# Low halves of split weights: an accumulating DMA in place of a subtraction

## The chip, the cores and the metric

The kernel runs on one core of a Trainium2 chip. The metric is device time in microseconds, from launch to end, of the whole program. The profile gives the span from the first to the last instruction of one execution, and times within it are counted from the start of that span.

## The reference

One layer of a bidirectional encoder for an input x of 1024 positions by 1024 channels, float32. The input is RMS-normalised and multiplied with one wide projection matrix; from its columns two branches are fed, an S5 state-space branch (512 channels) and a Hyena branch (1024 channels, two long filters applied in the frequency domain). Both are projected back, merged with sigmoid gates, projected once more, added to x and normalised.

```
xn = rmsnorm(h, norm_w[l])
proj = xn @ w_in[l]
u_s5, g_s5, p_hy, g_hy, m_logits = jnp.split(proj, SPLITS, axis=-1)
y_s5 = s5_mixer(u_s5, g_s5, ...) @ w_branch_s5[l]
y_hy = hyena_mixer(p_hy, g_hy, ...) @ w_branch_hy[l]
m = jax.nn.sigmoid(m_logits)
merged = m[..., :D_MODEL] * y_s5 + m[..., D_MODEL:] * y_hy
h = h + merged @ w_out[l]
return rmsnorm(h, final_norm_w)
```

## The kernel before

Products are made from halves. A float32 tile is split into a high half, which is the value rounded to the matmul format float32r, and a low half, which is the rest; a product is the sum of three passes: high by high, high weight by low input, low weight by high input.

A projection (`proj`, `projs`, line 529) computes 128 output columns for all 1024 positions. Its weights are one column block of 128 columns, taken as 8 blocks of 128 rows (4 for `s5_w_glu` and `w_branch_s5`). It has 16 matmuls in each of three passes (8 with 4 blocks), in the order high weight with `xh`, high weight with `xl`, low weight with `xh`; all go into one PSUM tile `pps`, of which there are two. There are 76 such column blocks, in the order that `weight_pools` (line 490) writes down: the S5 inputs and gates, the merge gates, the Hyena inputs, and the output matrices of the branches.

`prefetch` (line 502) keeps two column blocks ahead of use. For each it loads the raw block (`wraw`, 512 KB or 256 KB, three buffers, SyncE's queue), makes the high half on ScalarE (`whi`, line 510) and the low half by a subtraction (`wlo`, line 513). `whi` and `wlo` have two buffers each, so the halves of one block can be written when the block two before has been used. The subtraction is on GpSimd, except for nine of the last blocks, where it is on VectorE.

The stages, in the order of the span: the Hyena filters (to about 240 us, without projections), S5 inputs and the parameters of the S5 recurrence, four S5 blocks (`s5_block`, mostly VectorE, with projections in between on TensorE), the end of the S5 branch (`s5_tail`, with the small projections), the first forward transform (`hy_forward0`), the first inverse (`hy_inverse0`), the second forward (`hy_forward1`), the second inverse (`hy_inverse1`) and the output. In the transforms the planner weaves projections into the transform's own matmuls. `load_ic` (line 593) loads the constants of an inverse transform, 4 MB, when the forward transform's buffers are free.

The order of the instructions on each engine is not that of the program text: `tile.TileContext(nc, schedule_with_timeline_sim=True)` chooses it from priorities (program order) and from estimated times. At run time every engine and every queue works in that fixed order, and waits at the head of its queue.

Of the kernel before, what the change touches and what calls it, by code (L numbers as in the profile page):

```python
# [12 lines left out]
ALU = mybir.AluOpType  # L13
AF = mybir.ActivationFunctionType
# [86 lines left out]
class Trunk:  # L101
# [400 lines left out]
    def prefetch(self):  # L502

        nc = self.nc
        while (len(self.weights) < 2 or self.w_more) and self.order:
            name, c, nk = nxt = self.order.pop(0)
            raw = self.wr.tile([128, nk, 128], F, name="wraw")
            nc.sync.dma_start(out=raw, in_=self.I[name][0, :, c * 128:c * 128 + 128].rearrange("(k p) c -> p k c", p=128))
            hi, lo = self.w_more.pop() if self.w_more else self.weight_tiles(nk)
            nc.scalar.copy(out=hi, in_=raw)  # L510
            left = len(self.order)
            eng = nc.vector if left < 18 and left % 2 else nc.gpsimd
            eng.tensor_tensor(out=lo, in0=raw, in1=hi, op=ALU.subtract)  # L513
            self.weights.append((nxt, hi, lo))

    def weight_tiles(self, nk):
# [967 lines left out]
```

## Time and profile before

| | |
|---|---|
| median of 3 runs | 1487.98 us (1487.8 to 1488.49) |
| the profiled execution | 1488.18 us |
| its span, first to last instruction | 1486.4 us |
| mean granted TensorE clock | 0.963 of full speed |
| TensorE busy | 1358.1 us, 91% |
| VectorE busy | 1100.0 us, 74% |
| ScalarE busy | 447.0 us, 30% |
| GpSimd busy | 486.4 us, 33% |

Busy shares are means over stages with different limits; what a change in one stage is worth is read in that stage. In the rows PE is TensorE, DVE is VectorE, ACT is ScalarE, POOL is GpSimd, SP is SyncE; a name with a q behind it is that engine's queue. L513 is line 513 of the kernel.

### The profile page before, as it was taken

The numbers are of one execution on the slowest core, as the hardware profiler recorded it, in microseconds if no ns is written. First come the engines' busy times: TensorE is split into PE (matmuls) and PEld (weight loads), VectorE is DVE, ScalarE is ACT, GpSimd is POOL, SyncE is SP. The second block draws the span as 40 slices with busy tenths as digits, with TensorE's granted clock in tenths as the row PEclk, the third lists the DMA queues.
The fourth block names the chain that finished last, engine by engine and source line by source line (L and its number), as shares of the span: only waits on it lengthen the run. The fifth ranks groups of instructions, "written<-read, shape, count | busy, mean of one in ns | idle before, by whom it ended". The sixth has DMA issues, their size and how long they took to land. (4 is left out here: it accounts for less than half of the span.)

```text
span 1486.4 us, 19375 instructions
## 1 busy us (share of the span) xinstructions
PE 1358.1 (91%) x7219; PEld 1143.8 (77%) x7219; DVE 1100.0 (74%) x1963; ACT 447.0 (30%) x661; POOL 486.4 (33%) x306
## 2 busy tenths in 40 slices
PE   5888999998988989899999998999999944999998
PEld 3767888786867868688888776888888844978886
DVE  7999996899789887525479998454569994943532
ACT  4666662122222122232121211333321112511322
POOL 3756764114111111234223312245412111333222
PEclk9998999999999999899999999999999976999999
DMA  8221224622652323243853345645477669633432
GB/s 270 86 71 72 106 86 158 170 86 71 216 160 77 86 74 74 78 143 116 276 182 114 128 140 188 191 158 167 156 267 265 219 209 314 205 131 112 127 111 75
DMA packets 177673, 220.52 MB, mean 148 GB/s; under 512 B 21853, under 2 KB 142937, under 8 KB 174844
## 3 DMA queue, kind: packets, MB, share of 16 engines
q1 hardware_dynamic: 149212, 153.69, 33.8%
q10 hardware_dynamic: 27792, 62.45, 11.6%
q0 software_dynamic: 576, 3.15, 0.6%
q8 instruction: 57, 0.93, 0.3%
q14 instruction: 36, 0.29, 0.1%
HBM read 147.49 MB, written 76.82 MB: 151 GB/s over the span
## 5 line engine op out<-in xcount | busy, mean ns | idle before, releaser
L513 POOL TENSOR_TENSOR wlo<-wraw,whi 128x1024 fp32r<-128x1024 f32 (+1 forms) x67 | 169.6, 2533 | 588.1 <-PE pps L542 412.4
L542 PE MATMUL pps<-xh,whi 128*128 128x512 f32 x896 | 234.4, 408 | 11.5 <-DVE cv L566 11.5
L542 PE MATMUL pps<-xh,wlo 128*128 128x512 f32 x896 | 228.1, 401 | 0.0
L542 PE MATMUL pps<-xl,whi 128*128 128x512 f32 x896 | 226.0, 399 | 0.0
L542 PEld LDWEIGHTS pps<-xh,whi 128*128 128x128 f32 x896 | 169.9, 194 | 50.1 <-issue 12.3
L542 PEld LDWEIGHTS pps<-xh,wlo 128*128 128x128 f32 x896 | 169.2, 191 | 38.9
L542 PEld LDWEIGHTS pps<-xl,whi 128*128 128x128 f32 x896 | 167.9, 190 | 38.9 <-issue 0.2
L510 ACT CAST whi<-wraw 128x1024 fp32r<-128x1024 f32 (+1 forms) x76 | 74.7, 984 | 348.3 <-PE pps L542 276.1
L404 PE MATMUL po<-sh,fo 128*128 128x256 f32 x512 | 101.4, 292 | 6.0 <-DVE sh L111 5.1
L635 PEld LDWEIGHTS iv<-ic,y 128*128 128x128 f32 x752 | 96.5, 193 | 4.8 <-DVE y L113 2.3
L113 DVE TENSOR_TENSOR y<-yraw,y 128x512 fp32r<-128x512 f32 x64 | 61.7, 979 | 51.5 <-ACT y L109 51.2
L635 PE MATMUL iv<-ic,y 128*128 128x256 f32 (+1 forms) x752 | 98.4, 286 | 1.5 <-DVE y L113 1.5
L404 PEld LDWEIGHTS po<-sh,fo 128*128 128x128 f32 x512 | 84.3, 197 | 8.2 <-DVE sh L111 6.1
L357 POOL TENSOR_TENSOR acc<-acc,sq 128x512 f32<-128x512 f32 x56 | 76.3, 1362 | 25.0 <-ACT sq L342 22.8
L404 PE MATMUL po<-sl,fo 128*128 128x256 f32 x256 | 74.4, 291 | 1.0 <-DVE sl L113 1.0
L109 ACT CAST y<-yraw 128x512 fp32r<-128x512 f32 x64 | 39.3, 620 | 92.3 <-PE iv L635 54.1
L722 DVE TENSOR_TENSOR m<-m 128x512 f32<-128x512 f32 x64 | 53.0, 848 | 0.0
L404 PEld LDWEIGHTS po<-sl,fo 128*128 128x128 f32 x256 | 50.5, 197 | 2.3 <-DVE sl L113 1.5
L686 PE MATMUL fwo<-z,zc 128*128 128x256 f32 x384 | 50.1, 283 | 0.5 <-DVE x L716 0.5
L333 PE MATMUL g<-w3h,ha 128*128 128x512 f32 x64 | 33.0, 516 | 19.1 <-DVE e L338 17.3
L686 PEld LDWEIGHTS fwo<-z,zc 128*128 128x128 f32 x384 | 48.5, 191 | 1.6 <-DVE x L716 0.7
L336 ACT ACTIVATE e<-dec,negt 128x512 f32<-128x512 f32 x64 | 45.2, 716 | 10.6 <-DVE so L350 4.8
(437 smaller groups left out, 2685.1 us busy)
## 6 DMA issues: line engine op xcount, KB each, us to landing
wraw<-w_in SPq DMA_DIRECT2D x56, 512.0 KB, 4.6
kspec<-ko SPq DMA_DIRECT2D x32, 512.0 KB, 3.0
kt<-kspec SPq DMA_DIRECT2D x32, 512.0 KB, 3.3
d_y<-x ACTq DMA_DIRECT2D x32, 512.0 KB, 6.0
yraw<-d_y SPq DMA_DIRECT2D x64, 256.0 KB, 4.8
d_m<-cv ACTq DMA_DIRECT2D x16, 512.0 KB, 2.9
d_z<-z ACTq DMA_DIRECT2D x8, 1024.0 KB, 9.8
z<-d_z SPq DMA_DIRECT2D x8, 1024.0 KB, 10.9
```

The costliest lines, as they stand in the source:

```text
L109: nc.scalar.copy(out=hi, in_=src)
L113: e.tensor_tensor(out=lo, in0=src, in1=hi, op=ALU.subtract)
L333: nc.tensor.matmul(out=ps, lhsT=ha[:, tsl], rhs=w3h, start=True, stop=False)
L336: nc.scalar.activation(out=e, in_=decf, func=AF.Exp, scale=negt[:, tt:tt + 1])
L357: nc.gpsimd.tensor_tensor(out=acc, in0=acc, in1=sq, op=ALU.add)
L404: nc.tensor.matmul(out=po[:, part], lhsT=fo[a][:, 12 * (jj % 2) + b], rhs=sd[4 + i][d][:, part], start=n == 0 and part == 0, stop=n == 11 ...
L510: nc.scalar.copy(out=hi, in_=raw)
L513: eng.tensor_tensor(out=lo, in0=raw, in1=hi, op=ALU.subtract)
L542: nc.tensor.matmul(out=ps[:, hf * 512:hf * 512 + 512], lhsT=w[:, kc], rhs=part(x, kc, hf), start=a == 0 and p == 0 and kc == 0, stop=b == ...
L635: nc.tensor.matmul(out=dst, lhsT=lhsT, rhs=self.ic[b][:, j, cols], start=first, stop=last)
L686: nc.tensor.matmul(out=out, lhsT=zc[a][:, b], rhs=z[:, :, d, zi], start=start and n == 0, stop=stop and n == 3 * len(prods) - 1)
L722: nc.vector.tensor_tensor(out=m[:, part, :, 0], in0=m[:, part, :, 0], in1=m[:, part, :, 1], op=op)
```

## The change

The subtraction is replaced by two steps. ScalarE writes minus the high half into `wlo`, and a DMA on GpSimd's queue adds the raw block to it in place. The choice between VectorE and GpSimd goes away.

```
             nc.scalar.copy(out=hi, in_=raw)
-            left = len(self.order)
-            eng = nc.vector if left < 18 and left % 2 else nc.gpsimd
-            eng.tensor_tensor(out=lo, in0=raw, in1=hi, op=ALU.subtract)
+            nc.scalar.activation(out=lo, in_=hi, func=AF.Copy, scale=-1.0)
+            nc.gpsimd.dma_start(out=lo, in_=raw, accum_op=ALU.add)
             self.weights.append((nxt, hi, lo))
```

## Rows read from the trace of the kernel before

**Rows 1.** Stretches: start:end, length, busy PE PEld DVE ACT POOL, clock, DMA, GB/s.
```profile
345.00:610.00 265.00, 234.46 (x1298) 194.06 (x1297) 232.34 (x288) 56.92 (x70) 51.26 (x15) 0.93 0.37 103
790.00:902.00 112.00, 103.55 (x541) 86.16 (x540) 110.00 (x136) 21.52 (x26) 29.39 (x10) 0.98 0.38 129
902.00:937.00 35.00, 35.00 (x144) 28.07 (x144) 24.59 (x30) 7.92 (x8) 5.35 (x2) 0.95 0.72 236
...
1080.00:1100.00 20.00, 19.78 (x107) 16.67 (x106) 8.81 (x11) 4.48 (x6) 4.21 (x2) 1.00 0.89 319
1144.00:1231.00 87.00, 63.51 (x349) 54.49 (x347) 85.52 (x105) 13.30 (x14) 18.29 (x6) 0.88 0.67 230
1231.00:1248.00 17.00, 0.22 (x1) 0.22 (x2) 3.44 (x4) 0.80 (x2) 1.36 (x1) 0.50 1.04 342
```

**Rows 2.** Line 513, the subtraction: duration in ns min/median/max, first and last start.
```profile
L513 POOL TENSOR_TENSOR wlo<-wraw,whi x67: 1289/2407/11716, 242.2 to 1367.9; 128x1024 fp32r<-128x1024 f32 x55, 128x512 fp32r<-128x512 f32 x12
L513 DVE TENSOR_TENSOR wlo<-wraw,whi x9: 1211/1217/1225, 1030.0 to 1357.6; 128x1024 fp32r<-128x1024 f32 x9
```

**Rows 3.** Timeline of GpSimd: start, duration, instruction, idle time before and its releaser.
```profile
399.64 3.50 POOL L513 TENSOR_TENSOR wlo<-wraw,whi 128x1024 fp32r<-128x1024 f32 x1 [17.02 <-PE pps L542]
...
914.96 2.94 POOL L513 TENSOR_TENSOR wlo<-wraw,whi 128x1024 fp32r<-128x1024 f32 x1 [15.01 <-PE pps L542]
```

**Rows 4.** Timeline of VectorE in the S5 blocks.
```profile
400.80 3.42 DVE L1202 TENSOR_TENSOR di<-di,e 128x1024 f32<-128x1024 f32 x1
...
462.89 1.21 DVE L1202 TENSOR_TENSOR di<-di,e 128x1024 f32<-128x1024 f32 x1
...
583.76 2.28 DVE L1215 TENSOR_TENSOR_SCAN st<-a,dr 64x1023 f32<-64x1023 f32 x1
586.07 4.31 DVE L1217 TENSOR_TENSOR_SCAN st<-a,dr 64x1023 f32<-64x1023 f32 x1
```

**Rows 5.** What TensorE waited for, 330 to 620: total us, times, longest.
```profile
PE s5ps L1236 <- DVE sr L1223: 17.1, 3, 6.6
PE pps L542 <- DVE cv L566: 7.2, 1, 7.2
```

**Rows 6.** Timeline of VectorE in the first forward transform.
```profile
851.59 3.33 DVE L719 TENSOR_TENSOR m<-x,kt 128x1024 f32<-128x1024 f32 x1
...
898.24 2.25 DVE L722 TENSOR_TENSOR m<-m 128x512 f32<-128x512 f32 x1
```

**Rows 7.** The cast of line 510 on ScalarE: duration in ns min/median/max.
```profile
L510 ACT CAST whi<-wraw x76: 613/1052/1058, 241.1 to 1364.0; 128x1024 fp32r<-128x1024 f32 x64, 128x512 fp32r<-128x512 f32 x12
```

**Rows 8.** GpSimd's own DMA issues: busy us, mean ns of one.
```profile
L232 POOL DMA_DIRECT2D fo<-c_fo_hi x2 | 1.3, 632 | 0.0
```

**Rows 9.** DMA issues: queue, count, KB each, median us to landing.
```profile
wraw<-w_in SPq DMA_DIRECT2D x56, 512.0 KB, 4.6
...
wraw<-w_branch_s SPq DMA_DIRECT2D x8, 256.0 KB, 2.7
...
fo<-c_fo_hi POOLq DMA_DIRECT2D x2, 768.0 KB, 7.7
```

**Rows 10.** The chain that ended last, between 1215 and 1265: start, us, what.
```profile
1228.42 1.15 DVE m L720
...
1230.90 6.72 DMA ic<-c_ic_hi_d
1237.64 10.16 DMA yraw<-d_y
```

**Rows 11.** Timeline of TensorE: two small projections, then three large ones.
```profile
707.65 2.02 PE L542 MATMUL pps<-tyh,whi 128*128 128x512 f32 x8
...
713.25 2.02 PE L542 MATMUL pps<-tyh,whi 128*128 128x512 f32 x8
...
910.93 3.89 PE L542 MATMUL pps<-xh,wlo 128*128 128x512 f32 x16
...
933.33 3.66 PE L542 MATMUL pps<-xh,wlo 128*128 128x512 f32 x15
```

## The prediction

> **What bounds the kernel now.** I read the busy time by stage first, then what each engine waited for, then the chain of work that ended last, then single stretches of the timeline. The reader should see three kinds of stage in [rows 1]. From 902 to 937 and from 1080 to 1100 TensorE is saturated and VectorE has room; most of the span is like that. In three stretches it is not: the S5 blocks (345 to 610, TensorE busy 234 of 265 us, VectorE 232), the first forward transform (790 to 902, VectorE 110 of 112) and the second (1144 to 1231, VectorE 85.5 of 87, TensorE 63.5). Last come 17 us in which TensorE does nothing (1231 to 1248) and the DMA engines are full. ScalarE and GpSimd are nowhere near a bound. So work taken from GpSimd is worth only what it returns to VectorE or to TensorE's waits.
>
> It returns something, because the subtraction and VectorE get in each other's way. The subtraction that starts at 399.64 takes 3.50 us against a median of 2.41 [rows 2, 3], and the VectorE instruction that meets it takes 3.42 us; the same line undisturbed takes 1.21 [rows 4]. A scan that meets one takes 4.31 against 2.28 [rows 4]. Between 395 and 590 I count 11 such meetings, the first at 400.80 and the last at 586.07, with an excess of 1.5 to 2.2 us each and 22 us in sum. TensorE waits 24.3 us for VectorE in these blocks and at their end: 17.1 and 7.2 [rows 5].
>
> **What is removed.** 67 subtractions on GpSimd and 9 on VectorE [rows 2].
> S5 blocks: 22 us of VectorE's time go. VectorE's chain of a block and TensorE's waits alternate, so the relief comes through while TensorE still waits (24.3 us); but a faster VectorE will now and then stand before TensorE instead. Bounds 0 and 22; I take 18, because both the relief and the waits are larger than that.
> First forward transform: four subtractions meet VectorE between 842 and 902, the first at 851.59 and the last at 898.24 [rows 6], with an excess of 1.6 to 2.2 us each and 7.5 in sum; TensorE is idle for 8.5 us between 790 and 902 [rows 1]. Bounds 0 and 8.5; I take 6.
> Second forward transform: three VectorE subtractions of 1.22 us lie on a VectorE that is 98% busy [rows 1, 2], 3.6 in sum, and two on GpSimd fall into it, at 2.2 each at most by the meetings above. This chain decides when the constants of the last inverse transform are loaded [rows 10]. Bounds 3.6 and 8; I take 4.6, since these two meet VectorE only in part.
> In the saturated stages the removal is worth nothing: TensorE works there without a gap.
>
> **What is added on ScalarE.** One negated copy per weight tile, priced as the cast beside it: 1.05 us for eight blocks, 0.61 for four [rows 7]. 64 × 1.05 + 12 × 0.61 = 74.5 us on an engine that is under 25% busy in every stage of [rows 1]. It must wait until the low buffer is free, that is until the last pass of the projection two before has ended; GpSimd waited for that until now (914.96, 15 us of waiting [rows 3]). What stands behind it on ScalarE is the next evictions, which come from matmuls still ahead on TensorE, so they lose 1.05 us at most, and TensorE has a second PSUM buffer. I cost it at nothing; without that cover it would be 1 us for each of the 12 small projections and as many large ones in saturated stages, some 20 us.
>
> **What is added on GpSimd and the DMA engines.** 76 DMAs. Issue: the nearest row is a casting DMA from GpSimd, 0.63 us of the engine [rows 8]. Transfer: the same 512 KB from HBM took 4.6 us, 256 KB took 2.7, and GpSimd's own 768 KB loads 7.7 [rows 9]. An accumulation also reads the old low half, and no row shows one; I take 7.7 for 512 KB and half for 256 KB. Lower bound 4.6, upper bound 15.4, twice the row taken.
> Is that hidden? Follow one tile. The low buffer is free when the last pass of one projection ends, at 914.9 (the pass from 910.93; GpSimd starts at 914.96 [rows 3]), and the low half is read at 933.33, in the third pass of the second projection after: 18.4 us [rows 11]. An eviction (about 1.2), the negated copy (1.05) and the issue (0.6) leave 15.5 us for the transfer. For the small projections the period is 5.6 us (707.65 to 713.25 [rows 11]): 5.6 + 3.7 − 0.6 − 0.6 leaves 8.1. The prices taken, 7.7 and 3.9, fit with 7.8 and 4.2 to spare; the upper bound just fits twice. So no wait on TensorE.
> The raw buffer is given back some 5 us later than by a subtraction. SyncE's next weight load waits for it, and behind that stand the spectrum and constant loads. There are three raw buffers for two blocks kept ahead, so the raw block is there a projection early. I cost it at nothing; without that cover it is 5 us for each load that something waits for.
> The traffic is not free where the DMA engines are already full [rows 1]. At the 342 GB/s of 1231 to 1248, 512 KB are 1.5 us for one pass and 3.1 for two. Two transfers fall into 902 to 937 (0.72 busy), one into 1080 to 1100 (0.89), one into 1231 to 1248. The first pair costs 4 of its 6.1, because TensorE needs those constants only at the end of the stretch; the others cost 3 each. In sum 10; bounds 0 and 16 (three passes).
>
> The Trainium skill speaks against the change here: its page "SBUF — State Buffer", section "Who interferes with whom", says that a DMA issued from GpSimd can stall because VectorE's copies and tensor-scalar operations keep GpSimd from writing descriptors, while its tensor-tensor operations do not. What rows show is a subtraction held for 11.7 us instead of 2.4 [rows 2] under a dense run of VectorE tensor-tensor work; no row shows a descriptor write held. By that rule only the short copies would hold an issue and the sum stays; held as that subtraction was, it is the third rival.
>
> **The sum.** The profiled execution took 1488.18 us, 0.2 above the median shown. 1488.2 − 18 − 6 − 4.6 + 10 = 1469.6, so 1470. Its own range, with every term halfway to its bound, is 1460 (20, 7.3, 6.3 and 5) to 1485 (9, 3, 4 and 13). If each issue held up VectorE as a subtraction does, in proportion 0.63 to 2.41, a quarter of the 28.6 would be lost: 1477, inside that range.
>
> **Rivals.**
> 1. The S5 relief buys no time. For it: VectorE itself waited there, 265 − 232 = 33 us idle [rows 1], so it may only arrive earlier at TensorE's queue; the order on each engine is also chosen anew by the planner. Against it: 24.3 us of TensorE's waits name VectorE [rows 5]. Time: 1488.2 − 6 − 4.6 + 10 = 1487.6.
> 2. The low halves come late. The accumulation lands later than 15.5 us after its issue (8.1 for the small tiles). At 17 us each of about 22 large projections that run back to back (8 S5 inputs, 8 of the last matrix and some 6 between transforms, by the kernel's order) would wait 1.5, and each of 12 small ones 0.4: 1469.6 + 33 + 5 = 1508, and some 22 to 28 more for each further microsecond. Against it: it needs 3.7 times the plain load [rows 9].
> 3. The issue is starved as one subtraction was, 9.3 us (11.7 − 2.4) [rows 2]. Then 9.3 + 7.7 exceeds the 15.5 by 1.5 in the VectorE-bound stretches, with about 20 transfers (the 11, 4 and 5 of the terms above): 1469.6 + 30 = 1500. Against it: the median subtraction took 2.41, so long holds are rare.
>
> **How the numbers follow.** Forecast 0.60; rival 1 0.15; rival 2 0.15; rival 3 0.10. 0.2% is 3 us, about what a measurement of this kernel can tell from no change. All of the forecast and half of rival 1 lie below 1485: 0.67 faster. The middle of rival 1 is the same: 0.07. The rest of it and rivals 2 and 3 are slower: 0.26. The range goes from 1455, a little above the forecast's full bounds (1488.2 − 22 − 8.5 − 8 + 0 = 1449.7), to 1505, which takes in rivals 1 and 3 and the beginning of 2.
>
> **What would show it.** Right: VectorE's multiplications in the S5 blocks all at 1.2 us; TensorE's 17.1 us of waits there mostly gone; low-half passes that never wait; the constant load 4 to 5 us nearer to the end of the last forward transform's matmuls, its 17 us longer by 3. Wrong: TensorE waiting at low-half weight loads for GpSimd's queue, a landing time above 15 us, a new ScalarE wait before evictions, or a planner order that moves filler projections out of the S5 blocks.

## The result, and the profile after

The changed kernel takes 1446.64 us (median of 4, 1443.77 to 1448.17) where the kernel before, on the same chip, takes 1488.24 (1487.8 to 1489.76): a ratio of 0.9717, 95% interval 0.9698 to 0.9735, or 41.6 us less. The forecast was 1470. The profiled execution took 1447.77 us, its span 1445.9, 40.5 less than before.

First, where the 40.5 us come from. The table cuts both spans at the start of a first matmul: of the first small projection, of the first forward transform, of the first inverse one, and so on. A stage is the difference of two such starts.

| stage (us) | before | change | difference | forecast |
|---|---|---|---|---|
| up to the first small projection (S5 parameters and blocks) | 655.5 | 620.2 | -35.3 | -18 |
| small projections | 91.1 | 92.0 | +0.9 | 0 |
| first forward transform, projections behind it | 190.2 | 182.5 | -7.7 | -6 + 4 |
| first inverse transform, up to the second forward one | 155.8 | 154.1 | -1.7 | +3 |
| second forward transform, up to the inverse one's first matmul | 155.2 | 159.9 | +4.7 | -4.6 + 3 |
| second inverse transform | 142.1 | 140.6 | -1.5 | 0 |
| output | 96.5 | 96.6 | +0.1 | 0 |

So the miss is above all in the first line. Up to 296 the two kernels are within a microsecond. From 296 to the first small projection, the view of stretches (start:end, length, busy time and count of PE, PEld, DVE, ACT, POOL, then granted clock, DMA share, GB/s) says of the kernel before:

```profile
296.00:655.50 359.50, 328.96 (x1726) 271.04 (x1725) 290.12 (x562) 81.53 (x95) 73.16 (x24) 0.95 0.36 103
```

and of the changed kernel:

```profile
296.00:620.20 324.20, 319.04 (x1726) 263.32 (x1725) 244.63 (x533) 101.45 (x117) 25.36 (x24) 0.99 0.58 151
```

The same 1726 matmuls. TensorE stands still for 5.2 us in place of 30.5 (359.50 - 328.96), which is 25.4 of the 35.3; and the matmuls themselves take 319.0 us in place of 329.0, which is the other 9.9, at a granted clock of 0.99 in place of 0.95. VectorE's busy time falls from 290.1 to 244.6. Each of these numbers is of one profiled execution: in five of the kernels below that make the low halves of these blocks in the same way, one of them the change itself a second time, the first small projection starts at 621.2 to 624.9, so the stage's gain is 30.6 to 35.3 us. The waits of TensorE in the changed kernel, 290 to 660 (total us, times, longest), answer to [rows 5]:

```profile
PE pps L541 <- DVE cv L565: 3.2, 1, 3.2
PE s5ps L1235 <- DVE sr L1222: 1.9, 2, 1.4
PE pps L541 <- DMA wlo<-wraw: 0.5, 1, 0.5
```

17.1 and 7.2 have become 1.9 and 3.2. VectorE's instructions by shape in the S5 blocks (345 to 600; busy us, mean ns) answer to [rows 4]; all are now at the length of an undisturbed one:

```profile
L1216 DVE TENSOR_TENSOR_SCAN st<-a,dr 64x1023 f32<-64x1023 f32 x4 | 9.1, 2286 | 0.1
...
L1220 DVE TENSOR_TENSOR sr<-st,rr 128x1024 f32<-128x1024 f32 x4 | 4.9, 1222 | 0.1
L1201 DVE TENSOR_TENSOR di<-di,e 128x1024 f32<-128x1024 f32 x4 | 4.9, 1219 | 0.0
```

What the change adds, from the page's groups (busy us, mean ns | idle before, releaser) and its list of DMA issues (count, KB, median us to landing):

```profile
L512 POOL DMA_DIRECT2D wlo<-wraw x76 | 66.8, 879 | 717.8 <-ACT wlo L511 568.3
...
L511 ACT ACTIVATE wlo<-whi 128x1024 fp32r<-128x1024 f32 (+1 forms) x76 | 74.9, 985 | 20.6 <-PE pps L541 20.4
...
wlo<-wraw POOLq DMA_DIRECT2D x64, 512.0 KB, 5.8
```

And the chain that ended last, where the second forward transform ends, beside [rows 10] (1.15 us of VectorE's product, then 6.72 and 10.16 us of loads before):

```profile
1189.08 10.80 DMA ic<-c_ic_hi_d
1199.90 8.84 DMA yraw<-d_y
```

### The profile page after: what moved, and what is told of

It reads as the page before. It is cut to its first block, busy times and chain, and to the rows that moved or that the text cites. A ratio compares the mean times of both kernels' runs of the same rounds, so it can differ in the third digit from the quotient of the medians.

```text
span 1445.9 us, 19569 instructions
## 1 busy us (share of the span) xinstructions
PE 1343.9 (93%) x7219; PEld 1132.4 (78%) x7219; DVE 1009.2 (70%) x1954; ACT 515.7 (36%) x737; POOL 379.6 (26%) x315
## 3 DMA queue, kind: packets, MB, share of 16 engines
q1 hardware_dynamic: 149212, 153.69, 34.2%
q0 software_dynamic: 11520, 39.85, 14.6%
## 4 chain that ended last, share of the span: by engine, by line
PE 66%; DVE 14%; DMA 8%; issue 2%; ACTq 0%; ACT 0%; SPq 0%; DVEq 0%
PE pps L541 42%; PE iv L634 6%; PE ops L1384 6%; DMA d_y<-x 3%; PE po L404 2%; DMA zc<-c_zc_lo_d 2%; PE fwo L685 2%; PE pe L414 1%; PE fwe L685 1%; DVE st L1216 1%; PE zt L670 1%; DVE st L1214 1%; PE s5ps L1166 1%; DVE e L338 1%; DVE m L719 1%
## 5 line engine op out<-in xcount | busy, mean ns | idle before, releaser
L512 POOL DMA_DIRECT2D wlo<-wraw x76 | 66.8, 879 | 717.8 <-ACT wlo L511 568.3
L541 PE MATMUL pps<-xh,whi 128*128 128x512 f32 x896 | 229.1, 400 | 3.2 <-DVE cv L565 3.2
L541 PE MATMUL pps<-xh,wlo 128*128 128x512 f32 x896 | 223.9, 396 | 0.0
L541 PEld LDWEIGHTS pps<-xh,whi 128*128 128x128 f32 x896 | 165.9, 189 | 40.1 <-ACT wlo L511 3.6
L113 DVE TENSOR_TENSOR y<-yraw,y 128x512 fp32r<-128x512 f32 x64 | 52.8, 837 | 55.4 <-ACT y L109 54.9
L511 ACT ACTIVATE wlo<-whi 128x1024 fp32r<-128x1024 f32 (+1 forms) x76 | 74.9, 985 | 20.6 <-PE pps L541 20.4
L563 DVE SCALAR_TENSOR_TENSOR cv<-pps,cw,cv 128x1023 f32<-128x1023 f32 x24 | 30.7, 1280 | 30.4 <-ACT cv L562 30.4
```

Source lines behind the costliest of these rows:

```text
L113: e.tensor_tensor(out=lo, in0=src, in1=hi, op=ALU.subtract)
L511: nc.scalar.activation(out=lo, in_=hi, func=AF.Copy, scale=-1.0)
L512: nc.gpsimd.dma_start(out=lo, in_=raw, accum_op=ALU.add)
L541: nc.tensor.matmul(out=ps[:, hf * 512:hf * 512 + 512], lhsT=w[:, kc], rhs=part(x, kc, hf), start=a == 0 and p == 0 and kc == 0, stop=b == ...
```

## The experiments

Each is the changed kernel or the kernel before with a few lines edited in the function of the diff; `n` below is the index of the weight block, 0 to 75 (75 less what is left in the written-out order). Line numbers in their profiles are up to six higher than in the changed kernel. Times of the kernel before are those measured on the same chip with them.

**S5: is it the meeting of two engines?** Four kernels. The first puts the subtraction back as work that nothing reads, so that the low half is still made by the transfer:

```
             nc.gpsimd.dma_start(out=lo, in_=raw, accum_op=ALU.add)
+            if 5 <= n <= 22:
+                spare = self.wp.tile([128, 8, 60], R, name="spare", bufs=1)
+                for k in (0, 64):
+                    nc.gpsimd.tensor_tensor(out=spare, in0=raw[:, :, k:k + 60], in1=hi[:, :, k:k + 60], op=ALU.subtract)
```

> The change, with a GpSimd subtraction (15/16 of the columns, in two instructions) written to a spare tile that nothing reads, for the 18 weight blocks that fall between 296 and 613 of the kernel before. Theory A (the S5 stretch gave back 35 us because the subtraction slows the VectorE instruction that meets it, TensorE then waits 4 to 7 us, and its granted clock falls after each wait): VectorE's operations there take 2 to 3 us again, TensorE's waits go from 5 back to 20 to 30 us, the first small projection goes from 620 back to about 650, in all 1472 to 1485 us. Rival B (the gain comes from another order of the instructions, or from low halves that no longer wait for their buffer on GpSimd): no stretch moves by over 3 us, 1444 to 1450.

1469.65 against 1489.35 us, ratio 0.9864 (0.985 to 0.9879): 19.7 of the 41.6 us are left, 22 are gone again. The second has `nc.gpsimd.tensor_copy(out=spare, in_=raw[:, :, k:k + 60])` in that place.

> As the run with the spare subtraction, but a copy with one operand in its place. If any SBUF work of GpSimd slows VectorE, the time returns in proportion to the copy's length beside the subtraction's: with a copy of half the length, about 1460 to 1466. If only an operation with two operands does it: 1444 to 1450. Rival B: 1444 to 1450 as well.

1449.59 us, 0.9732 (0.9715 to 0.9749), which the interval of the change (0.9698 to 0.9735) does not exclude; its first small projection, at 624.3, lies among those of the change. The third makes the low half on GpSimd from ScalarE's negated copy, for all blocks:

```
             nc.scalar.activation(out=lo, in_=hi, func=AF.Copy, scale=-1.0)
-            nc.gpsimd.dma_start(out=lo, in_=raw, accum_op=ALU.add)
+            nc.gpsimd.tensor_tensor(out=lo, in0=lo, in1=raw, op=ALU.add)
```

> ScalarE's negated copy stays; the accumulating transfer becomes a GpSimd addition of the raw tile in SBUF, for all 76 blocks. Theory A: the 35 us of the S5 stretch return, some 7 of the first forward transform and up to 4 of the second too, and the 6 us that the transfers cost go: 1446.6 + 35 + 7 + 4 - 6 = 1487, in the range 1478 to 1492. Rival B (what counted was that the low buffer's wait and the negation moved to ScalarE, or the order): 1437 to 1447, the change without the cost of its transfers.

1494.35 us, 1.0032 (1.0021 to 1.0044): all of the gain is lost, and 5 us more. The fourth puts the subtraction on VectorE: both new lines go, and `nc.vector.tensor_tensor(out=lo, in0=raw, in1=hi, op=ALU.subtract)` stands in their place.

> All 76 subtractions on VectorE, none on GpSimd, no transfers: no meetings, but 1.22 us of VectorE each (0.61 for the small ones). Theory A (what costs is the meeting, some 2 us of VectorE and 1 to 9 us of GpSimd each, more than the work itself): S5 gains some of its 35 us in spite of 18 x 1.22 = 22 us more VectorE work there, first small projection at 635 to 650, 1470 to 1484 in all. Rival (VectorE's total load is what counts, and the meeting is just the work): first small projection at 655 or later, 1488 to 1500.

1456.69 us, 0.9789 (0.9772 to 0.9806): better than expected. The rows of the S5 stretch, 296 to the first small projection, in this order of kernels:

```profile
296.00:641.50 345.50, 326.16 (x1724) 269.23 (x1723) 273.54 (x529) 101.46 (x117) 95.71 (x60) 0.96 0.55 141
```

```profile
296.00:624.30 328.30, 320.82 (x1725) 264.94 (x1724) 255.21 (x535) 101.44 (x117) 63.03 (x59) 0.98 0.58 150
```

```profile
296.00:656.30 360.30, 328.59 (x1727) 270.82 (x1726) 288.30 (x562) 101.80 (x117) 77.21 (x25) 0.95 0.36 103
```

```profile
296.00:619.80 323.80, 319.28 (x1737) 264.35 (x1736) 272.50 (x581) 78.98 (x93) 6.07 (x2) 0.99 0.40 115
```

Read them by TensorE's idle time, length minus the first busy time: 19.3, 7.5, 31.7 and 4.5 us, beside 30.5 before and 5.2 with the change. An operation of GpSimd with two operands brings waits back (14 of the 25 us that went, in the first kernel), whether something needs its result or not; with the third kernel everything is back that was removed, although ScalarE still makes the negated copy and the stretch holds the same matmuls. The fourth kernel decides what the price is: VectorE is 28 us busier than with the change (272.5 against 244.6) and TensorE waits even less. So it was not VectorE's load, it was what a meeting does to the instruction on TensorE's path. One of the first kernel's meetings, on GpSimd and on VectorE (start, duration):

```profile
425.63 3.41 POOL L516 TENSOR_TENSOR spare<-wraw,whi 128x480 fp32r<-128x480 f32 x2 [16.39 <-issue]
```

```profile
424.60 1.22 DVE L1114 TENSOR_TENSOR pi<-ci,ppr 128x1024 f32<-128x1024 f32 x1
425.74 2.24 DVE L1189 TENSOR_TENSOR rt<-ra,rb 128x1024 f32<-128x1024 f32 x1
427.90 2.22 DVE L1113 TENSOR_TENSOR pr<-pr,pt 128x1024 f32<-128x1024 f32 x1
```

1.22 undisturbed, 2.24 and 2.22 in the meeting. In the copy's kernel the same instructions take 1.49 to 1.61, and it is the copies that drag:

```profile
419.44 5.49 POOL L516 CAST spare<-wraw 128x480 fp32r<-128x480 f32 x4 [12.65 <-DMA wraw<-w_in]
```

```profile
419.43 1.22 DVE L1189 TENSOR_TENSOR rt<-ra,rb 128x1024 f32<-128x1024 f32 x1
420.56 1.61 DVE L1113 TENSOR_TENSOR pr<-pr,pt 128x1024 f32<-128x1024 f32 x1
422.09 1.60 DVE L1190 TENSOR_TENSOR ri<-ri,rt 128x1024 f32<-128x1024 f32 x1
```

**How much of it did the forecast leave out?** The change for a part of the blocks, the old subtractions (GpSimd, or VectorE for some of the last 18) for the others; here `5 <= n <= 10`, the blocks whose subtractions fell between 296 and 380, then `5 <= n <= 22`:

```
+            if 5 <= n <= 10:
                 nc.scalar.activation(out=lo, in_=hi, func=AF.Copy, scale=-1.0)
                 nc.gpsimd.dma_start(out=lo, in_=raw, accum_op=ALU.add)
+            else:
+                left = len(self.order)
+                eng = nc.vector if left < 18 and left % 2 else nc.gpsimd
+                eng.tensor_tensor(out=lo, in0=raw, in1=hi, op=ALU.subtract)
```

> The change for the 6 blocks whose subtractions fell between 296 and 380, which the forecast left out of its S5 term, the subtractions of before for the other 70. Theory A: the first small projection comes 8 to 14 us earlier, since two TensorE waits of 2.9 and 3.5 us, some 10 us of slower VectorE work and one drop of the granted clock lie there: 1475 to 1481 of 1489.3. If that stretch is worth nothing, as the forecast had it: 1487 to 1491.

1479.78 against 1488.51 us, 0.9939 (0.9924 to 0.9953). The row of the stretch, 9.3 us shorter than before:

```profile
296.00:646.20 350.20, 325.96 (x1727) 269.04 (x1727) 275.79 (x564) 86.85 (x101) 54.62 (x24) 0.96 0.41 115
```

> The change for the 18 blocks between 296 and 613 alone, the subtractions of before for the other 58. If the gain of the S5 stretch stands by itself: 1488.2 - 35 = 1453, give or take 3, with the first small projection at 620. If the S5 term is what was forecast (18): 1470. If the gain needs the change elsewhere too (order, transfers): above 1475.

1456.47 against 1489.35 us, 0.9781 (0.9765 to 0.9797), half a microsecond above the expected 1453 plus 3; the first small projection starts at 621.3, 34.2 earlier than before. So 18 of 76 blocks bring 33 of the 41.6 us.

**The clock.** That matmuls take longer after a wait can be seen in the kernel before around the wait of 6.2 us that ends at 422.4 (stretches of 4 us; the eighth column is the granted clock):

```profile
416.00:420.00 4.00, 0.20 (x1) 0.00 (x0) 3.97 (x4) 1.28 (x1) 0.00 (x0) 1.00 1.01 330
420.00:424.00 4.00, 1.62 (x6) 1.52 (x7) 4.00 (x5) 0.00 (x0) 0.00 (x0) 0.64 0.36 94
424.00:428.00 4.00, 4.00 (x11) 3.13 (x10) 3.97 (x4) 0.00 (x0) 0.00 (x0) 0.51 0.00 0
428.00:432.00 4.00, 4.00 (x33) 3.78 (x33) 1.36 (x2) 0.60 (x1) 0.00 (x0) 1.00 0.00 0
```

TensorE is granted its full 2.4 GHz, stands still, and after it works at 0.51 of that, the 1.2 GHz level, until about 428. Is that VectorE's doing too? A kernel meant for something else answers it. It adds plain loads from HBM to a spare tile, for the blocks of the second forward transform:

```
             nc.gpsimd.dma_start(out=lo, in_=raw, accum_op=ALU.add)
+            if 61 <= n <= 70:
+                spare = self.wp.tile([128, 3, 128], F, name="spare", bufs=1)
+                for k in (0, 3):
+                    nc.gpsimd.dma_start(out=spare, in_=self.I[name][0, :, c * 128:c * 128 + 128].rearrange("(k p) c -> p k c", p=128)[:, k:k + 3])
```

> The change, and for the 10 blocks from the constant load of the second forward transform to the next one 384 KB each of plain loads from HBM to a spare tile that nothing reads, on GpSimd's queue. If the traffic makes that stretch slow: some 1.1 us more for each at 342 GB/s, half to all of it on the chain, 1451 to 1458. If it is the raw buffer given back late (SyncE's weight loads wait 82 us there for the accumulation, 26 us for the subtraction before): 1445 to 1449.

1453.2 us, 0.9769 (0.9752 to 0.9786), but not for the reason expected: the loads wait for no weight block, and all 20 were issued between 239 and 328, in front of accumulations on GpSimd's queue. The second forward transform took 156.7 us, so the run says nothing about traffic there. What it shows is one low half that came late, TensorE's wait of 4.6 us for it near 311, and the clock after that wait:

```profile
PE pps L547 <- DMA wlo<-wraw: 5.2, 2, 4.6
```

```profile
312.00:316.00 4.00, 0.42 (x1) 0.42 (x2) 3.78 (x28) 1.36 (x2) 0.77 (x1) 0.67 0.89 187
316.00:320.00 4.00, 4.00 (x10) 3.04 (x10) 3.76 (x28) 0.00 (x0) 0.76 (x1) 0.50 0.64 185
320.00:324.00 4.00, 4.00 (x18) 3.26 (x17) 3.86 (x28) 1.98 (x2) 0.76 (x1) 0.97 0.28 92
```

Ten matmuls in 4 us where the next 4 us hold 18. A transfer was waited for, VectorE had no part in it, and the level fell all the same. In the rows of the S5 stretch (1724 to 1737 matmuls) TensorE's busy time goes with its idle time: 319.0 to 320.8 us beside 4.5 to 7.5 us idle, 326.0 and 326.2 beside 24.2 and 19.3, 328.6 and 329.0 beside 31.7 and 30.5. So the 9.9 us are the price of the waits, whoever causes them.

**The first forward transform.** The change for `46 <= n <= 53` alone:

> The change for the 8 blocks of the first forward transform alone, the subtractions of before for the other 68. If that stage's gain stands by itself (190.2 us before and 182.5 with the change, from its first matmul to the first inverse transform): 7 to 10 us, so 1479 to 1482 of 1488.5. The forecast's term was 6, bounds 0 and 8.5. If the transfers eat it: 1485 or more.

1481.38 against 1487.91 us, 0.9953 (0.9939 to 0.9968): 6.5 us. The stage takes 182.3 us (929.3 - 747.0), as with the full change.

**The second forward transform.** First the old subtractions for its ten blocks, the change for the others (`if not 61 <= n <= 70`):

> The change for 66 blocks, the subtractions of before for the 10 whose low halves are made from the constant load of the second forward transform to the next constant load. Theory C (in the second forward transform the transfers cost more than the subtractions did: the stretch from its first matmul to the first of the inverse transform took 155.2 us before and 159.9 with the change): that stretch returns to 155 to 156.5, and the kernel takes 1441 to 1444. Rival (the stretch is longer because it starts earlier against loads that don't): it stays at 158 to 160, 1446 to 1450.

1443.37 against 1488.51 us, 0.9697 (0.9682 to 0.9712); the stage takes 156.2 us (1205.6 - 1049.4). To tell whether the kernel as a whole is better, the change and this kernel ran again on one chip:

> The change as it is, again, as the measure for the two kernels beside it: 1444 to 1449.

> The change with the subtractions of before for the 10 blocks of the second forward transform, again, beside the change on the same chip. If the transfers cost there what the stages showed (159.9 us against 156.2): 2.5 to 5 us below the change. If that was the spread of one profiled execution: within 1.5 us of it.

1445.8 (1444.48 to 1446.13) and 1444.57 us (1439.79 to 1449.73); ratios to before 0.9706 (0.9693 to 0.972) and 0.97 (0.9679 to 0.9722). The stage is shorter again, 156.2 against 160.4 us, but the two kernels can't be told apart. Then the reason for the longer stage. What waits there in the changed kernel, 1048 to 1209, on SyncE and on VectorE:

```profile
SPq L508 <- DMA wlo<-wraw: 82.1, 9, 14.4
...
DVE ke L703 <- PE fwe L685: 14.0, 1, 14.0
DVE x L714 <- DMA d_y<-x: 8.0, 8, 1.9
```

SyncE's weight loads wait 82 us for the raw buffer, and VectorE 8.0 us for stores that have not left their tile (1.9 us in all before). One kernel reads the addend from HBM, so that the raw buffer is free after the cast:

```
-            nc.gpsimd.dma_start(out=lo, in_=raw, accum_op=ALU.add)
+            nc.gpsimd.dma_start(out=lo, in_=self.I[name][0, :, c * 128:c * 128 + 128].rearrange("(k p) c -> p k c", p=128), accum_op=ALU.add)
```

> The change with the accumulation read from HBM in place of the raw tile, so that the raw buffer is free after the cast, as early as could be; the DMA engines move the same bytes. If the second forward transform is slower because SyncE's loads stand behind a raw buffer given back late: its stretch falls from 159.9 to 156 or less, 1441 to 1444. If it is the traffic: 159 to 162, 1445 to 1450. The prediction costed the late raw buffer at nothing.

1454.07 us, 0.9772 (0.975 to 0.9793), outside both. The stage takes 157.0 us, 2.9 less. But S5 takes 6.4 more and the transfers land later, from rows of 512 bytes in 73472 packets (11520 with the change):

```profile
q0 software_dynamic: 73472, 39.85, 21.0%
...
wlo<-w_in POOLq DMA_DIRECT2D x56, 512.0 KB, 7.3
```

```profile
PE pps L547 <- DMA wlo<-w_in: 3.7, 2, 3.4
```

The other kernel leaves the raw buffer alone and adds traffic in the right place, by transfers that read the high half:

```
+            if 61 <= n <= 70:
+                spare = self.wp.tile([128, 3, 128], R, name="spare", bufs=1)
+                for k in (0, 3):
+                    nc.gpsimd.dma_start(out=spare, in_=hi[:, k:k + 3])
```

> The change, with two more transfers of 192 KB each, from the high half to a spare tile that nothing reads, for the 10 blocks of the second forward transform. The high half exists only after the cast, so these can't be issued ahead. If traffic makes the stretch slow: its 159.9 us grow by 3 to 8, and the kernel by as much. If it is the raw buffer given back late: within 2 us of the change.

1451.24 us, 0.974 (0.9727 to 0.9753), 5.4 above the change on the same chip. The stage takes 163.5 us (160.4), SyncE's wait for the accumulations is 70.4, less than in the change (79.0 on the same chip), and VectorE waits for stores twice as long (5.4 there):

```profile
DVE x L720 <- DMA d_y<-x: 10.7, 9, 1.9
```

The chain that ended last shows it too. In this stage of the kernel before, one store of x lies on it, 4.18 us long; in the changed kernel there are seven, 46.6 us in all, among them

```profile
1067.53 8.39 DMA d_y<-x
...
1098.74 8.55 DMA d_y<-x
...
1173.09 9.48 DMA d_y<-x
```

and with the added traffic eight, 54.5 us. So traffic is one cause, by way of the stores. How much it costs is known only roughly, since a stage is read from one execution each: five kernels whose second forward transform is made as in the change took 156.7 to 160.8 us there (25.9 to 46.6 us of stores on the chain), six with the old subtractions 155.1 to 156.2 (none or one store). Late raw buffers as a second cause are not shown: the 157.0 us of the kernel that reads from HBM lie among those of the change, and the plain loads' kernel came to 156.7 with 79.8 us of SyncE's waits. Nor is the work better left on one engine there: the stage took 162.2 us with VectorE's subtractions alone and 162.1 with GpSimd's additions.

**A better version?** Two mixtures, VectorE's subtractions (no meetings, no traffic) for the first 46 blocks and the old subtractions for 61 to 70; the change for 46 to 60 and 71 to 75 in the one, for 46 to 53 alone in the other, and VectorE for the rest there:

```
+            if 46 <= n <= 60 or n > 70:
                 nc.scalar.activation(out=lo, in_=hi, func=AF.Copy, scale=-1.0)
                 nc.gpsimd.dma_start(out=lo, in_=raw, accum_op=ALU.add)
+            else:
+                eng = nc.vector if n < 46 or n % 2 == 0 else nc.gpsimd
+                eng.tensor_tensor(out=lo, in0=raw, in1=hi, op=ALU.subtract)
```

> VectorE subtractions for the first 46 blocks, the change from the first forward transform to the first inverse one, the subtractions of before in the second forward transform, the change for the last 5. By the stages of the runs so far (619.8 to the first small projection with VectorE alone, 89.9 from there to the transform, 180 to 182 for the transform, then as with the old subtractions in the second transform): 1437 to 1443. If VectorE's subtractions push other work into the first transform, as they may have with VectorE alone (197.6 us there): 1446 to 1458.

> As the mixed version before, but the change for the 8 blocks of the first forward transform alone; VectorE subtractions in the first inverse transform and for the last blocks too. If the 145.8 us of the first inverse stage with VectorE alone come from transfers that are gone: 1432 to 1438. If they come only from projections done earlier: 1438 to 1446, no better than the first mixed version.

1446.47 us, 0.9722 (0.9707 to 0.9736), and 1445.74 us, 0.9714 (0.9698 to 0.973). Neither differs from the change. The first forward stage takes 188.2 and 188.1 us (182.5 with the change) and the first inverse one 149.6 and 148.2 (154.1), as with VectorE alone (197.6 and 145.8): projections were done earlier. The first of the two stages holds 985 and 984 matmuls in place of 944, and TensorE is never idle in it; together the two take 337.8 and 336.3 us, with the change 336.6. No version beat the change by more than the measurement can tell.

## Why the prediction was wrong

**S5 blocks, -18, bounds 0 and 22: the step that failed; -35.3.** The mechanism was right, the term was too small in two ways. TensorE's waits of [rows 5] fell from 24.3 to 5.1 us, 19.2, close to the 18. But the excess was counted from 395 on, and of the waits only those of the blocks; two more, of 2.9 and 3.4 us, end at 361 and 366. VectorE comes late to them because five subtractions between 302 and 350 each held one of the many short instructions that work out the S5 parameters, 0.2 us long, for 2.28 to 2.40 us, some 11 us in sum. The subtraction that takes 11.7 us [rows 2] is no part of that: there it was GpSimd that was held, while eight instructions of VectorE ran at 1.22. In the kernel before:

```profile
302.74 2.40 POOL L513 TENSOR_TENSOR wlo<-wraw,whi 128x1024 fp32r<-128x1024 f32 x1 [8.74 <-PE pps L542]
302.89 2.31 DVE L953 TENSOR_TENSOR sx<-mag,ur 128x32 f32<-128x32 f32 x1
...
358.74 11.72 POOL L513 TENSOR_TENSOR wlo<-wraw,whi 128x1024 fp32r<-128x1024 f32 x1 [8.76 <-PE pps L542]
...
360.19 1.22 DVE L1108 TENSOR_TENSOR nr<-nr,nt 128x1024 f32<-128x1024 f32 x1
```

These 6.3 went too, and the six blocks there are worth 9.3 by themselves, 6.3 of idle time and 3.0 of busy time. And a wait was priced at its own length. What it does to the clock behind it was left out, although [rows 1] show 0.93 for the S5 blocks, and 0.95 for 902 to 937, without a gap but behind a wait of 4.4 us, beside 1.00 from 1080 to 1100: 9.9 us. 19.2 + 6.3 + 9.9 = 35.4. The upper bound, VectorE's excess, was no bound, because it left out the stretch before and the clock.

**First forward transform, -6: right.** TensorE's idle time there went from 8.4 us (190.20 - 181.75) to 2.1 (182.50 - 180.38), and the change in that stage alone is worth 6.5 us. That the stage and the next one lost 9.4 in sum is 6.3 of idle time and 3.1 of busy time on the same 1826 matmuls, with the granted clock of the first stage at 0.98 before and 0.99 after.

**Second forward transform, -4.6: wrong; +4.7 with the loads at its end.** VectorE did get the relief, 123.8 us busy in place of 132.4, and spent it waiting: 14.0 us for TensorE where 5.8 were before, and 8.0 for stores where 1.9 were. What failed here is the path. The forecast let VectorE's chain decide when the last constants are loaded; with the change stores of x stand on the path, 46.6 us for 4.2. The forecast counted the DMA engines' load as a price for constant loads only, and not for stores that hold a VectorE tile. The size is uncertain: against the 155.2 before, the five kernels made as the change there show 1.5 to 5.6.

**Transfers, +10, bounds 0 and 16: too much.** Of the 4 us at 902 to 937 nothing shows: TensorE's only wait in that stage, 2.1 us, is for the forward transform's own constants. Of the 3 at 1080 to 1100 the load in the chain (another one of the same transform) shows 2.2 (16.63 for 14.43), and its stage is 1.7 shorter, with 8 matmuls fewer. The last 3 were right: 10.80 + 8.84 against 6.72 + 10.16 is 2.8.

**The rest.** The issue takes 0.88 us for the estimated 0.63, and 512 KB land in 5.8 us for the 7.7 taken, 256 KB in 4.4 for 3.9; TensorE waits 0.5 us for a low half in the small projections, for a transfer that landed after 8.2 us, so the slack of 8.1 us there was as named and just used up. The sign "a landing time above 15 us" came twice, 21.0 us for the transfer issued at 393.5 and 15.3 for the one at 1038.2, and TensorE waited for neither: the first landed at 414.5 and was read at 417.6. The kernel that reads from HBM, at 7.3, already waits 3.7. The negated copies cost nothing, as forecast. The raw buffer costed at nothing stays open: SyncE waits 56 us more for it in the second transform (82.1 against 26.2 before), and what of that reaches the end was not separated. Of the signs named, VectorE's lengths, TensorE's waits and the longer idle stretch came; the constant load did not move nearer to the transform's last matmul (28.8 us behind it, 26.5 before).

**Rivals.** That the relief buys no time is refuted by the 33 us of the S5 blocks alone. Late low halves cost 0.5 us in this kernel, and 5.2 as soon as other loads stood on GpSimd's queue. No issue was held: of 76 the longest took 1.20 us.

In sum, by the table's stages: -35.3 for -18 in S5; -8.5 for +1 from the small projections to the second transform (transfers that cost next to nothing for 7, and the clock); +4.7 for -1.6 in the second transform; -1.4 for 0 behind it. 17.3 + 9.5 - 6.3 + 1.4 = 21.9, which is 40.5 less the 18.6 forecast. The other 1.1 us up to the 23 between the forecast and the median is what the profiled execution took above the median.

## What to carry to other kernels

Where two engines slow each other, don't price the meeting by the busier engine's load: find the chain of instructions that the bound engine waits for, and take away what can meet it there; 28 us more work on VectorE cost nothing in S5, while 2.4 us of GpSimd's at the wrong moment put some 2 us into the chain each. A wait of TensorE costs its length and then some of its clock, here 9.9 us on 25.4, so look at the granted clock of a stretch before bounding what its waits are worth. Work moved to the DMA engines is free only where no store or load holds a buffer that a bound engine needs next.

## What the runs showed of the hardware that was not expected

- A GpSimd subtraction, with two operands in SBUF, and a VectorE instruction with two slow each other (1.22 to 2.24 us), and either can be held as long as the other is at work: VectorE instructions of 0.2 us took as long as the subtraction (2.31 beside 2.40), also a copy with one operand (2.32), and a subtraction took 11.7 us in place of 2.4 beside a dense run of VectorE. A GpSimd copy slows VectorE's products much less (1.49 to 1.61 for 1.22) while it is itself dragged out: two copies alone take 1.24 us, in a meeting with scans up to 5.01. The Trainium skill's page "SBUF — State Buffer", section "Who interferes with whom", says that a VectorE instruction with two inputs in SBUF contends with a GpSimd instruction that reads SBUF. The trace agrees for the subtraction.
- Issuing an accumulating transfer from GpSimd took 0.85 to 1.20 us, 76 times, and VectorE's groups in the S5 blocks kept their undisturbed lengths beside it; the accumulation of 512 KB within SBUF landed in 5.8 us in the median, about as fast as a plain load from HBM (4.7 in the same kernel).
- With waits of 4.6 to 6.2 us the granted clock fell to 0.50 or 0.51 behind the wait, and was back at 0.97 to 1.00 in the stretch after it. It did so behind a wait for VectorE and behind one for a transfer alike.
